# Running prompt rows and sample rows half a layer out of step in a four-layer diffusion trunk

## The chip, the cores and the metric

The program runs on all 8 cores of one Trainium2 chip (two dies of four cores). Each core does the same work on its own rows with its own copy of the program. The time is that of the slowest core, in device microseconds (us), from its first to its last instruction.

An eight-core program has a second, slower state in some executions: the cores of one die, sometimes of both, show a lower granted TensorE clock and the time grows (here by 3 to 16%). Such runs are named slow below and are left out of every comparison.

## The reference, cut to what matters

Four layers act on two groups of rows that share all weights. Prompt rows attend only to prompt rows. Sample rows use their own rows and cached context tensors. Even layers mix with a short convolution beside a neighbourhood attention, odd layers with window pooling beside a latent attention. Every layer ends in an MLP with squared relu, and six modulation vectors per layer come from a matrix `ada_w`.

```python
def sq_relu_mlp(h, w1, w2):               # 1024 -> 4096 -> 1024
    a = jax.nn.relu(h @ w1)
    return (a * a) @ w2

for l in range(DEPTH):                    # DEPTH = 4
    sh1p, sc1p, g1p, sh2p, sc2p, g2p = ada_mod(s_ctx, ada_w[l], ada_b[l])
    sh1s, sc1s, g1s, sh2s, sc2s, g2s = ada_mod(s_lat, ada_w[l], ada_b[l])
    hp = modulate(yp, norm1_g[l], sh1p, sc1p)
    hs = modulate(ys, norm1_g[l], sh1s, sc1s)
    # ... mix_p from hp alone, mix_s from hs and the caches (cut) ...
    yp = yp + g1p * mix_p
    ys = ys + g1s * mix_s
    yp = yp + g2p * sq_relu_mlp(modulate(yp, norm2_g[l], sh2p, sc2p), mlp_w1[l], mlp_w2[l])
    ys = ys + g2s * sq_relu_mlp(modulate(ys, norm2_g[l], sh2s, sc2s), mlp_w1[l], mlp_w2[l])
```

The two groups never read one another. That is what lets one run ahead of the other. Per core there are 512 prompt rows and 1024 sample rows, held as three blocks of 512 tokens: block 0 is prompt, blocks 1 and 2 are sample.

## The kernel before: the parts that matter

The kernel lists all operations with what they read and write. A scheduler in Python then plays the program through with a modelled duration for each operation, and so fixes, when the program is built, the order of the instructions on every engine. The program gives each engine its list in that order, with waits on semaphores; nothing in it picks another order at run time. The modelled duration of a weight load is this:

```python
DMA_LAT = 1.9
...
            if nd.kind == "dma":
                dma_free = max(dma_free, st + 1.0) + nd.nbytes      # one queue; nbytes holds us
                fin = dma_free + self.DMA_LAT - 1.0
...
        def DMA(q, pairs, reads, writes, sem, out=False, key=None):
            fns = [lambda h, o=o, i_=i_: h.dma_start(out=o, in_=i_) for (o, i_) in pairs]
            t = sum(R(o).nbytes() / (0.17e6 if R(o).dtype != R(i_).dtype else 0.25e6) for (o, i_) in pairs)
```

Weights lie in HBM as float32 and are cast to bfloat16 by the DMA. A tile of 1 MB (as it lands) thus costs 6.2 us of modelled queue time plus 1.9 us of latency. A tile goes to a slot; a slot is filled again only when all readers of its last contents are done:

```python
            def fill(self, srcs, after=(), key=None):
                self.b = P.renew(self.b)
                s = "ws%d" % (nsl[0] % 24)
                nsl[0] += 1
                DMA("pool", [(self.w[:, 0:src.shape[1], c0:c0 + nc_], src) for (c0, nc_, src) in srcs], list(after), [self.b], s, key=key)
                return self.w, self.b

        WT = [Slot(w=sb("WT%d" % s, (128, 8, 512), BF16)) for s in range(2)]
```

Where the plan leaves TensorE idle for more than 0.9 us, the scheduler puts in matmuls on a tile of ones, called fillers here, which are meant to keep its clock up:

```python
            if e == "pe" and self.warm is not None and st - free[e] > self.WARM_MIN:      # 0.9 us
                self.fill_gap(nodes, free[e], st, bank_free, bank_users)
```

All three blocks go through each layer together. In the MLP one fetched tile serves all three, and hidden values are squared on ScalarE (ACT) and masked on VectorE (DVE):

```python
            order = [M[0], M[1], WT[0], WT[1]] * 3 + [WT[0], WT[1], M[0], M[1]]
            ...
                    for tb in range(3):
                        for j in range(4):
                            ...
                            MMK(pt[:], [(w[:, kc, j * 128:(j + 1) * 128], hT[:, kc, blk(tb)]) for kc in range(8)],
                                [bw] + bh[tb], [pt.b])
                            mk, bm = msk.next()
                            ACT(mk[:], pt[:], AF.Square, [pt.b], [bm])
                            STT(hq[:, jj, blk(tb)], pt[:], 0.0, mk[:], ALU.is_gt, ALU.mult, [pt.b, bm], [bhq[jj][tb]])
...
        for l in range(depth):
            if l % 2:
                odd_layer(l, ada[l][1])
            elif l > 0:
                even_layer(l)
            mlp(l, l + 1 == depth, ada[l + 1][0] + (ada[l + 1][1] if l % 2 else []))
```

`MMK` is a group of eight accumulating matmuls, `STT` a DVE operation with a scalar and two tensors, `TT` and `TS` DVE operations with two tensors and with scalars.

## Time and profile before

| | before |
|---|---|
| fast runs (us) | 2498.53, 2502.76 (and 2496.78 beside the changed kernel) |
| slow run (us) | 2726.35 |
| spans of the cores in the profiled run | 2478.9 to 2500.3 |
| mean granted TensorE clock of the cores | 0.983 to 0.990 |
| weight tiles of the MLP, 1 MB each | 64 |
| fillers | 1095 |
| bytes moved by DMA | 212.01 MB |

These lines are from the page of the slowest core: busy time of TensorE, its busy share and that of ACT and of the DMA engines in 40 slices (9 means 90% or more), the DMA total, and the chain of work that ended last, as shares of the span.

```profile
PE 2345.9 (94%) x14913; PEld 1166.4 (47%) x14913; DVE 1183.4 (47%) x1748; ACT 1070.9 (43%) x1607; POOL 256.6 (10%) x344
...
PE   4999899999998899999999988999998879999999
...
ACT  2666741121567764111256774121136777412210
...
DMA  9969673333217758667534549343322391433322
...
DMA packets 204842, 212.01 MB, mean 85 GB/s; under 512 B 46320, under 2 KB 191472, under 8 KB 202736
...
PE 79%; DMA 9%; ACT 5%; issue 3%; DVE 2%; POOL 1%; ACTq 0%; POOLq 0%; DVEq 0%; SPq 0%
```

TensorE (PE) looks full. The rows below tell more: where ACT shows 5 to 7 (the attention of each layer) PE drops to 8 or 7 and the DMA row swings between 1 and 9; where ACT shows 1 to 2 (the MLPs) PE is at 9, and in the MLPs of layers 0, 2 and 3 the DMA is down to 2 to 4.

Three stretches of core 1 show the contrast. The columns are the stretch, its length, busy time and instruction count of each engine, the granted clock, the DMA share and GB/s.

```profile
core 1: us, PE busy (x) PEld busy (x) DVE busy (x) ACT busy (x) POOL busy (x), PEclk, DMA share, GB/s
400.00:425.00 25.00, 25.00 (x146) 11.78 (x145) 10.32 (x17) 2.98 (x5) 1.62 (x2) 1.00 0.47 75
800.00:825.00 25.00, 21.99 (x378) 14.97 (x375) 8.54 (x16) 22.38 (x26) 2.63 (x3) 1.00 0.82 164
875.00:900.00 25.00, 21.77 (x268) 13.06 (x266) 5.60 (x8) 23.77 (x25) 0.00 (x0) 1.00 0.01 1
```

The first is MLP: PE is full and nothing else is. The third is attention in layer 1: ACT is busy 23.77 of 25 us, PE waits for it, and the DMA is idle. The change wants to fill the third kind with work of the first.

### The profile page before, as it was taken

How to read it: one execution, taken by the hardware profiler on the slowest of the kernel's cores; microseconds unless marked ns; L12 is line 12 of the kernel's file. 1: busy time of each engine (PE TensorE's matmuls, PEld its weight loads, DVE VectorE, ACT ScalarE, POOL GpSimd, SP SyncE). 2: the span in 40 equal slices, each digit the busy share in tenths (PEclk: the TensorE clock that was granted, in tenths of full speed). 3: DMA queues.
4: the chain of work that ended last, by engine and by line, in shares of the span. 5: the costliest groups of instructions: out<-in, count | busy, mean ns of one | idle time of the engine just before them, and what ended most of it. 6: DMA issues, size and time to landing. Idle time of an engine off the chain costs nothing.

```text
span 2500.3 us, 39661 instructions; the slowest of 8 cores (2478.9 to 2500.3 us)
## 1 busy us (share of the span) xinstructions
PE 2345.9 (94%) x14913; PEld 1166.4 (47%) x14913; DVE 1183.4 (47%) x1748; ACT 1070.9 (43%) x1607; POOL 256.6 (10%) x344
## 2 busy tenths in 40 slices
PE   4999899999998899999999988999998879999999
PEld 3454444444445544444444544444444455444444
DVE  2556554444656245444465655444455533544443
ACT  2666741121567764111256774121136777412210
POOL 3200100000014000000031001000001310000000
PEclk9999999999999999999999999999999999999999
DMA  9969673333217758667534549343322391433322
GB/s 172 166 92 195 108 113 61 51 51 51 74 36 125 130 78 109 85 84 97 63 76 54 122 87 136 57 61 51 51 57 70 62 158 40 67 52 52 52 45 101
DMA packets 204842, 212.01 MB, mean 85 GB/s; under 512 B 46320, under 2 KB 191472, under 8 KB 202736
## 3 DMA queue, kind: packets, MB, share of 16 engines
q0 software_dynamic: 176992, 148.39, 43.6%
q1 hardware_dynamic: 27664, 61.09, 7.6%
q8 instruction: 123, 2.02, 0.3%
q14 instruction: 63, 0.52, 0.1%
HBM read 334.07 MB, written 22.15 MB: 142 GB/s over the span
## 4 chain that ended last, share of the span: by engine, by line
PE 79%; DMA 9%; ACT 5%; issue 3%; DVE 2%; POOL 1%; ACTq 0%; POOLq 0%; DVEq 0%; SPq 0%
PE psall L638 79%; ACT arena L662 3%; DMA yT<-ada_w 3%; DMA WT<-even_w_out 1%; DMA WT<-even_w_in 1%; DMA WT<-ada_w 1%; DMA yT<-odd_w_in 1%; DMA arena<-ada_w 1%; DVE ntmp L684 1%; POOL rtmp L673 1%; DVE arena L673 1%; DMA yT<-xT 1%; ACT rstd L662 1%; ACT hT L662 1%; PE psall L646 0%
## 5 line engine op out<-in xcount | busy, mean ns | idle before, releaser
L662 ACT ACTIVATE arena<-psall 128x512 f32<-128x512 f32 (+6 forms) x675 | 434.7, 651 | 1043.4 <-PE psall L638 1033.5
L638 PE MATMUL psall<-arena,WT 128*128 128x512 bf16 x2688 | 587.5, 380 | 10.4 <-DMA WT<-even_w_out 6.7
L638 PE MATMUL psall<-hT,arena 128*128 128x512 bf16 x2520 | 559.3, 382 | 7.2 <-ACT hT L662 7.2
L684 DVE SCALAR_TENSOR_TENSOR yT<-psall,mod,yT 128x512 f32<-128x512 f32 x480 | 359.3, 750 | 428.0 <-PE psall L638 427.8
L638 PE MATMUL psall<-arena 128*128 128x65 bf16 (+7 forms) x3272 | 470.2, 293 | 44.0 <-ACT arena L662 24.2
L684 DVE SCALAR_TENSOR_TENSOR arena<-psall,arena 128x512 bf16<-128x512 f32 x384 | 265.3, 691 | 400.1 <-ACT arena L662 399.7
L638 PE MATMUL psall<-hT,WT 128*128 128x512 bf16 x1872 | 424.9, 382 | 5.8 <-ACT hT L662 4.3
L638 PEld LDWEIGHTS psall<-arena,WT 128*128 128x128 bf16 x2688 | 262.7, 98 | 326.3 <-issue 12.8
L638 PEld LDWEIGHTS psall<-hT,arena 128*128 128x128 bf16 x2520 | 246.9, 98 | 306.2 <-issue 17.0
L638 PEld LDWEIGHTS psall<-arena 128*128 128x128 bf16 (+1 forms) x3272 | 237.5, 99 | 249.9 <-issue 77.9
L638 PEld LDWEIGHTS psall<-hT,WT 128*128 128x128 bf16 x1872 | 181.8, 98 | 218.4 <-issue 12.4
L662 ACT ACTIVATE arena<-psall,rk 128x1024 bf16<-128x1024 f32 x160 | 166.7, 1118 | 34.9 <-PE psall L638 34.4
L684 DVE SCALAR_TENSOR_TENSOR ntmp<-yT,A,nrstd 128x512 f32<-128x512 f32 x192 | 135.9, 746 | 20.6 <-ACT nrstd L662 14.0
L662 ACT ACTIVATE hT<-ntmp,mod 128x512 bf16<-128x512 f32 x176 | 121.4, 718 | 40.9 <-DVE ntmp L684 40.1
L662 ACT ACTIVATE nsq<-yT 128x1024 bf16<-128x1024 f32 x55 | 58.0, 1055 | 165.7 <-PE psall L638 113.0
L684 DVE SCALAR_TENSOR_TENSOR arena<-psall,cst_sb,rstd 64x512 bf16<-64x512 f32 (+1 forms) x90 | 67.3, 748 | 64.7 <-ACT rstd L662 62.6
L726 POOL DMA_DIRECT2D WT<-mlp_w x32 | 28.2, 881 | 541.8 <-PE psall L638 541.5
L726 POOL DMA_DIRECT2D arena<-mlp_w x32 | 28.2, 880 | 539.1 <-PE psall L638 532.6
L1535 PE MATMUL psall<-ones 128*128 128x128 bf16 x1095 | 71.1, 222 | 0.0
L662 ACT ACTIVATE rstd<-rstd 128x512 f32<-128x512 f32 (+2 forms) x92 | 64.7, 703 | 8.5 <-ACT rstd L662 0.4
L638 PE MATMUL psall<-hT,yT 128*128 128x512 bf16 x288 | 68.0, 379 | 0.0
L1535 PEld LDWEIGHTS psall<-ones 128*128 128x128 bf16 x1095 | 65.4, 99 | 4.7
(111 smaller groups left out, 1285.9 us busy)
## 6 DMA issues: line engine op xcount, KB each, us to landing
arena<-mlp_w POOLq DMA_DIRECT2D x32, 1024.0 KB, 10.5
WT<-mlp_w POOLq DMA_DIRECT2D x32, 1024.0 KB, 9.9
yT<-ada_w POOLq DMA_DIRECT2D x24, 1024.0 KB, 11.7
arena<-ada_w POOLq DMA_DIRECT2D x22, 1024.0 KB, 16.7
arena<-rpbx SPq DMA_DIRECT2D x64, 240.0 KB, 2.8
ysc<-yT SPq DMA_DIRECT2D x5, 2048.0 KB, 6.8
yT<-ysc SPq DMA_DIRECT2D x10, 1024.0 KB, 7.6
yT<-xT SPq DMA_DIRECT2D x3, 2048.0 KB, 14.7
```

What stands on the lines that cost most here:

```text
L638: h.matmul(R(out), lhsT=lhsT, rhs=rhs, start=start, stop=stop, skip_group_check=skip))
L662: return lambda h: h.activation(out=R(out), in_=R(in_), func=func, **kw)
L673: P.add(eng, [lambda h: h.tensor_tensor(out=R(out), in0=R(in0), in1=R(in1), op=op)], reads, writes, vdur(fsize(out), eng, isb(out, in0, in ...
L684: P.add("dve", [lambda h: h.scalar_tensor_tensor(out=R(out), in0=R(in0), scalar=scalar, in1=R(in1), op0=op0, op1=op1)], reads, writes, vdu ...
L726: fns = [lambda h, o=o, i_=i_: h.dma_start(out=o, in_=i_) for (o, i_) in pairs]
L1535: P.warm = lambda h, o: h.matmul(o, lhsT=ones[:, :], rhs=ones[:, :], start=True, stop=True)
```

## The change

Its intent: the prompt runs half a layer ahead. In phase A of a layer the sample's attention runs beside the prompt's output projection and half of the prompt's MLP (320 matmuls of 512 columns, 68 us at the 212 ns of the trace, PE work that needs little of ACT). In phase B the sample catches up with its projection and its MLP, and the next layer's prompt projections and attention run beside the second half of that. One fetched MLP tile can no longer serve all three blocks in the first two quarters, so those are fetched twice.

The core of the diff, with cuts marked by dots:

```diff
-        for l in range(depth):
-            if l % 2:
-                odd_layer(l, ada[l][1])
-            elif l > 0:
-                even_layer(l)
-            mlp(l, l + 1 == depth, ada[l + 1][0] + (ada[l + 1][1] if l % 2 else []))
+        for l in range(depth):
+            if l == 0:
+                e, Hp = even_first()
+            else:
+                e, Hp = (odd_sample if l % 2 else even_sample)(l, p)     # these call phase_a
+            p = phase_b(l, odd_src if l % 2 else even_src(e), Hp)
 ...
+        def phase_a(l, src_p):
+            T = l * 200
+            out_proj(l, [0], src_p, T - 0.5 if l else 20, zone=[6, 7])
+            Hp = hidden(Arena(0), [0])
+            slots = [WT[0], WT[1]] * 4
+            eA, eB = [], []
+            if l % 2 and l + 1 < depth:
+                X = Slot(Arena(4096))
+                ADA["slot"] = lambda nt: X
+                eA, eB = ada[l + 1]
+            for qd in range(2):
+                mlp_q(l, qd, [0], Hp, slots, T + 30 + qd, zone=[6, 7], tmr=ntr, extra=eB if qd else eA)
+            return Hp
 ...
+        def phase_b(l, src_s, Hp):
+            T = l * 200 + 100
+            out_proj(l, [1, 2], src_s, T)
 ...
+                if nxt_odd:
+                    par = Arena(8848)
+                    PW, PB = Slot(par), Slot(par, n=160)
+                    ADA["slot"] = lambda nt: PW
+                    eA, eB = ada[l + 1]
+            mlp_q(l, 2, [0, 1, 2], H, slots, T + 10, extra=eA + eB[:1],
+                  tmr=None)
 ...
+            mlp_q(l, 3, [0, 1, 2], H, slots, T + 20, extra=eB[1:], tail=tail_p)
 ...             (the next layer's prompt projections and attention, keys T + 21 to T + 28)
+            mlp_q(l, 0, [1, 2], H, slots, T + 30)
+            mlp_q(l, 1, [1, 2], H, slots, T + 40, tail=tail_s)
```

Two smaller parts travel with it. The squared relu is computed in another way, and the scheduler may not let the backlog of weight loads grow beyond 10 modelled us:

```diff
-                            mk, bm = msk.next()
-                            ACT(mk[:], pt[:], AF.Square, [pt.b], [bm])
-                            STT(hq[:, jj, blk(tb)], pt[:], 0.0, mk[:], ALU.is_gt, ALU.mult, [pt.b, bm], [bhq[jj][tb]])
+                            RELU(pt)          # in place in PSUM, on ACT or DVE, whichever the plan has free
+                            ACT(hq[:, half * 4 + j, :], pt[:], AF.Square, [pt.b], [bhq[half * 4 + j]])
 ...
+    DMA_AHEAD = 10.0
 ...
+                    if nd.kind == "dma" and nd.nbytes > 1.0 and dma_free - self.DMA_AHEAD > st:
+                        st = dma_free - self.DMA_AHEAD
```

The prompt's own half MLP uses a third form, a `max` on DVE and a product on DVE or POOL. Small rotary products may go to either of DVE and POOL, and more token blocks are spilled to HBM and reloaded.

## The prediction

> **What bounds the kernel now.** TensorE, but less tightly than its 94% busy share says. In the MLP stretches (365-668, 985-1275, 1580-1870, 2210-2480 us of the windows view) 117-118 matmuls of 512 columns start in 25 us: one per 212 ns, granted clock 1.00. Nothing can be gained there. The Trainium skill ("TensorE: Matmul & The Clock Gate", Back-to-back issue gap) gives N/2.4 + 2.5 ns for an isolated gap; the trace agrees within 2%. "Trainium Kernel Development and Optimization" (Performance Expectations) warns that matmul busy time is a bad metric; here too: at 825-850 us PE is 22.3 us busy, yet streams only 16.3 us of columns.
>
> Pricing every matmul of the trace at columns/2.4 GHz (27 ns at least), the program streams 2206 us; fillers (the 1095 matmuls on a tile of ones) cost another 59 us of otherwise idle PE. So 294 of 2500 us are not useful streaming. About 70 lie before 90 us (first weights) and 6 at the end. The other ~218 us lie in the mixers: ~41 us in layer 0 (175-375), ~63 in layer 1 (668-985), ~36 in layer 2 (1400-1580), ~75 in layer 3 (1870-2210). There ACT paces (87.7 of 105 us at 800-905; 1.118 us per exp of 128x1024 against ~0.67 us of matmuls), norm chains leave gaps, and the chain of waits shows DMA stalls of 9-20 us on ada_w, even_w_out and odd_w_in.
>
> **What the change does.**
> - Matmul work is unchanged: 2206 us.
> - Each sample attention gets the prompt's out-projection (64 matmuls, 14 us) and half its MLP (256 matmuls, 55 us) as filler: ~69 us of independent PE work per layer, against 36-75 us lost there. The next layer's prompt projections and attention go beside the sample's MLP.
> - Squared relu becomes relu in PSUM, then square: two passes as before, ~0.6-0.7 us each against 1.7 us of matmuls; free.
> - Weights are fetched again: 32 MLP tiles, 8 out-projection tiles, and layers 1-3's mixer weights for two groups: ~54 MB more, plus ~16 MB of spill and reload. Moved bytes 212 -> ~280 MB, DMA share 51% -> ~66%. A 1 MB tile costs ~7 us when the DMA is saturated (~150 GB/s, 825-850 us).
> - Worst stage: layer 1's mixer, with 8 MLP, 2 out, 12 ada tiles and the mixer's own: I estimate ~215 us of DMA against ~225 us of PE. Late tiles stall the fixed order of PE there.
>
> **On the critical path.** Of the ~218 us I expect ~125 recovered: filler covers attention and norm gaps, but DMA lateness and transitions leave ~90 us (25 per mixer in layers 0, 1 and 3, 15 in layer 2). Start and end stay ~75 us. 2206 + 75 + 92 = 2373 us, 5% faster. Range 2310 to 2445. Faster by over 2%: 0.89; within 2%: 0.08; slower: 0.03.
>
> **What would show it.** Useful streaming unchanged at ~2206 us; fillers fall from 1095 to under 600; no stretch where ACT is nearly full while PE streams under 70%; 512-column matmuls still every 212 ns in the MLP; mlp_w issues 64 -> 96; DMA share near 66%. In the chain of waits, ACT's 5% falls below 3%; DMA keeps at least its 9%, which now makes most of the loss. PE in the chain: 79% -> over 84%.
>
> **What would make it wrong.** (a) DMA late under 30% more bytes: the PE order is fixed, so the filler itself stalls attention; then 2430 or more. (b) A two-bank PSUM zone and two weight slots for the prompt's MLP throttle the filler. (c) The denser PE is granted a lower clock. (d) Better: gaps really vanish and residual falls to 40 us: 2320.

## More of the kernel before

What PE waited for on core 1 (us in total, number of waits, the longest):

```profile
PE psall L638 <- ACT arena L662: 25.7, 85, 1.8
PE psall L638 <- DMA WT<-ada_w: 24.5, 2, 17.9
...
PE psall L638 <- DMA arena<-ada_w: 8.3, 4, 3.9
PE psall L638 <- DMA yT<-ada_w: 6.5, 6, 1.9
```

The 24.5 us on `WT<-ada_w` are the first weights of the program; every kernel below has them. Added up over the whole list, PE waited 42.1 us for ACT, 50.3 us for DMA, 23.0 us for DVE and 14.5 us for GpSimd (POOL). Last, how long a weight tile took from its issue to its landing on the slowest core (count, size, median us):

```profile
arena<-mlp_w POOLq DMA_DIRECT2D x32, 1024.0 KB, 10.5
WT<-mlp_w POOLq DMA_DIRECT2D x32, 1024.0 KB, 9.9
yT<-ada_w POOLq DMA_DIRECT2D x24, 1024.0 KB, 11.7
```

The order of the instructions was planned for 8.1 us of an unloaded queue; this becomes the main point later. For an unloaded queue that is not far off: of the 106 tiles of `mlp_w` and `ada_w` that core 1 issued after 100 us, 40 had no other transfer in flight and landed in 8.7 us (median). The other 66 took 12.1 us, and one in ten of those 19 us or more.

## The result, and the profile after

| | before | after |
|---|---|---|
| fast runs (us) | 2496.78, 2498.53, 2502.76 | 2540.97, 2542.30 |
| slow runs (us) | 2726.35 | 2785.65, 2880.91 |
| spans of the cores in the profiled run | 2478.9 to 2500.3 | 2469.3 to 2539.4 |
| granted clock of the cores | 0.983 to 0.990 | 0.971 to 0.983 |
| MLP weight tiles, 1 MB each | 64 | 96 |
| fillers | 1095 | 716 |
| bytes moved by DMA (MB) | 212.01 | 285.63 |

The changed kernel is right, and slower: the ratio is 1.0169, with a 95% interval of 1.0139 to 1.0199. A ratio here is the mean time of one kernel's fast runs over that of the other's fast runs of the same rounds, so it is not quite the ratio of the medians that are quoted. That is within 2%, but the interval excludes any gain, and the prediction was 2373 us.

The same lines of the page, slowest core again:

```profile
PE 2326.9 (92%) x14291; PEld 1151.0 (45%) x14534; DVE 1020.7 (40%) x1550; ACT 1219.2 (48%) x1848; POOL 322.5 (13%) x412
...
PE   5879889989899988999999998999999999899998
...
ACT  2536744243555667424443775153156376852322
...
DMA  9975896669566688734696966965976636353352
...
DMA packets 279703, 285.63 MB, mean 112 GB/s; under 512 B 70240, under 2 KB 264544, under 8 KB 276064
...
PE 70%; DMA 20%; issue 3%; ACT 3%; DVE 2%; POOL 1%; another core or an unknown queue 0%; DVEq 0%; ACTq 0%; POOLq 0%; SPq 0%
```

ACT's work is spread more evenly, as intended: its row seldom falls to 1 now. The DMA row has lost its long stretches of 3. In the chain, DMA went from 9% to 20%, and PE from 79% down to 70%. (This core's trace lacks 243 matmul records, 14291 against 14534 weight loads; sums are therefore taken from core 1.)

Core 1, four stretches, columns as before:

```profile
core 1: us, PE busy (x) PEld busy (x) DVE busy (x) ACT busy (x) POOL busy (x), PEclk, DMA share, GB/s
850.00:875.00 25.00, 17.76 (x124) 8.48 (x122) 11.34 (x21) 5.17 (x9) 4.85 (x7) 0.86 1.12 224
950.00:975.00 25.00, 18.40 (x246) 11.41 (x247) 2.66 (x6) 20.66 (x21) 0.87 (x1) 0.91 0.84 121
1050.00:1075.00 25.00, 25.00 (x118) 11.29 (x117) 0.00 (x0) 17.09 (x29) 0.87 (x1) 1.00 0.31 43
1400.00:1425.00 25.00, 25.00 (x117) 11.33 (x116) 20.74 (x30) 22.40 (x37) 5.26 (x6) 1.00 1.44 175
```

The last line is the change as it was meant: ACT busy 22.4 of 25 us and PE full, with 117 matmuls of 512 columns. The first is what came with it: PE, ACT, DVE and POOL all far from full, the clock down to 0.86, and the DMA saturated (I read shares above 1 as saturated). Of the 94 stretches of 25 us between 100 and 2450 us of core 1, 15 had a DMA share of 0.85 or more before; after, 31 of 95 have.

What PE waited for on core 1, and how long tiles took to land on the slowest core:

```profile
PE psall L641 <- DMA WT<-ada_w: 25.4, 2, 18.3
PE psall L641 <- DMA WT<-mlp_w: 24.7, 6, 7.4
PE psall L641 <- DMA arena<-ada_w: 23.9, 17, 4.2
PE psall L641 <- ACT arena L665: 19.9, 53, 3.4
PE psall L641 <- DMA arena<-odd_w_in: 10.9, 4, 3.1
```

```profile
WT<-mlp_w POOLq DMA_DIRECT2D x64, 1024.0 KB, 10.8
arena<-ada_w POOLq DMA_DIRECT2D x38, 1024.0 KB, 13.4
arena<-mlp_w POOLq DMA_DIRECT2D x32, 1024.0 KB, 10.6
```

The medians to landing are little above those of before. What grew is the number of tiles that share the queue: on core 1, counted as before, 115 of 138 in place of 66 of 106. They took 11.7 us in the median (one in ten 19 us or more), the 23 others 8.6 us.

Over the whole list the waits for DMA grew from 50.3 to 103.8 us, while those for ACT fell from 42.1 to 29.5 us. The eight cores agree: this sum is 73.1 us on core 5, which has the shortest span (2469.3 us), and 129.6 us on core 0, which has the longest (2539.4 us). One such wait in full, from the timeline of core 1 (start, duration, engine, instruction; in brackets the idle time before it and what ended it):

```profile
850.47 0.94 POOL L739 DMA_DIRECT2D WT<-mlp_w  x1 [2.68 <-PE psall L649]
...
860.14 0.61 PE L649 MATMUL psall<-ident,arena 128*128 128x128 bf16 x8
...
860.96 0.87 POOL L739 DMA_DIRECT2D WT<-mlp_w  x1 [2.20 <-PE psall L649]
...
867.51 1.86 PE L641 MATMUL psall<-hT,WT 128*128 128x512 bf16 x4 [6.76 <-DMA WT<-mlp_w]
```

A tile of the prompt's MLP, the filler of the plan, is issued at 850.47. PE runs out of other work at 860.75 and reads the tile at 867.51, 17 us after the issue. The plan counts 8.1 us for a tile that need not queue. PE's list is fixed, so the attention work behind those matmuls waits too: the filler has become the stall.

To see all of the loss I paired the starts of successive matmuls on core 1, took columns/2.4 GHz + 2 ns as the useful part of each interval (27 ns at least), and put the rest down to the clock or to what ended the wait. The time of fillers is the whole time until the next useful matmul starts. (The two kernels with thin tiles and with the slower plan are experiments, below; the rest, some 35 us of each, is start, end and gaps too small to assign.)

| us on core 1 | before | after | after, thin tiles | after, slower plan |
|---|---|---|---|---|
| useful streaming | 2214 | 2214 | 2214 | 2214 |
| fillers | 121 | 79 | 73 | 122 |
| slow clock | 32 | 45 | 10 | 20 |
| waits for ACT | 36 | 27 | 27 | 32 |
| waits for DVE and POOL | 30 | 24 | 21 | 25 |
| waits for DMA | 24 | 87 | 10 | 25 |

The change as a whole, the new relu included, did give back time: fillers −42 us, ACT −9 us, POOL and DVE −6 us. Waits for DMA took 63 us of it and the slower clock 13 us. Core 1 is 15 us longer as a result; the slowest core (core 0) 39 us longer.

### The profile page after: what moved, and what is told of

Read it like the earlier page. It is cut to its first block, busy times and chain, and to the rows that moved or that the text cites. A ratio compares the mean times of both kernels' runs of the same rounds, so it can differ in the third digit from the quotient of the medians.

```text
span 2539.4 us, 38663 instructions; the slowest of 8 cores (2469.3 to 2539.4 us)
## 1 busy us (share of the span) xinstructions
PE 2326.9 (92%) x14291; PEld 1151.0 (45%) x14534; DVE 1020.7 (40%) x1550; ACT 1219.2 (48%) x1848; POOL 322.5 (13%) x412
## 2 busy tenths in 40 slices
DMA packets 279703, 285.63 MB, mean 112 GB/s; under 512 B 70240, under 2 KB 264544, under 8 KB 276064
## 4 chain that ended last, share of the span: by engine, by line
PE 70%; DMA 20%; issue 3%; ACT 3%; DVE 2%; POOL 1%; another core or an unknown queue 0%; DVEq 0%; ACTq 0%; POOLq 0%; SPq 0%
PE psall L641 70%; DMA arena<-ada_w 8%; DMA WT<-mlp_w 3%; DMA yT<-even_w_in 2%; ACT arena L665 2%; DMA arena<-rpbx 2%; DMA arena<-odd_w_in 1%; DMA WT<-ada_w 1%; DMA yT<-ada_w 1%; DMA arena<-PA 1%; DVE arena L676 1%; DMA WT<-even_w_out 1%; ACT rstd L665 1%; DMA nak_out<-arena 0%; POOL rtmp L676 0%
## 5 line engine op out<-in xcount | busy, mean ns | idle before, releaser
L641 PE MATMUL psall<-arena,WT 128*128 128x512 bf16 x2866 | 657.2, 383 | 19.8 <-DMA WT<-mlp_w 12.8
L665 ACT ACTIVATE arena<-psall 128x512 bf16<-128x512 f32 (+7 forms) x631 | 411.3, 659 | 230.3 <-PE psall L641 181.5
L665 ACT ACTIVATE psall<-psall 128x512 f32<-128x512 f32 x320 | 186.4, 582 | 483.4 <-PE psall L641 482.8
L641 PE MATMUL psall<-arena 128*128 128x65 bf16 (+8 forms) x2940 | 368.6, 275 | 27.8 <-ACT arena L665 17.3
L641 PE MATMUL psall<-hT,WT 128*128 128x512 bf16 x1462 | 344.3, 387 | 27.4 <-DMA WT<-mlp_w 15.0
L641 PEld LDWEIGHTS psall<-arena 128*128 128x128 bf16 (+1 forms) x2960 | 200.8, 98 | 189.3 <-issue 45.3
L641 PEld LDWEIGHTS psall<-hT,WT 128*128 128x128 bf16 x1504 | 146.8, 99 | 202.7 <-issue 42.1
L665 ACT ACTIVATE arena<-psall,rk 128x1024 bf16<-128x1024 f32 (+1 forms) x224 | 196.9, 934 | 74.2 <-PE psall L641 68.8
L641 PE MATMUL psall<-hT,yT 128*128 128x512 bf16 x697 | 167.5, 385 | 17.8 <-DMA yT<-even_w_in 14.7
L641 PEld LDWEIGHTS psall<-hT,yT 128*128 128x128 bf16 x704 | 68.7, 99 | 99.2 <-issue 24.1
L691 DVE SCALAR_TENSOR_TENSOR arena<-psall,cst_sb,rstd 64x512 bf16<-64x512 f32 (+2 forms) x102 | 76.3, 749 | 82.2 <-ACT rstd L665 70.9
## 6 DMA issues: line engine op xcount, KB each, us to landing
WT<-mlp_w POOLq DMA_DIRECT2D x64, 1024.0 KB, 10.8
arena<-ada_w POOLq DMA_DIRECT2D x38, 1024.0 KB, 13.4
```

Of the source, the lines that this page charges most:

```text
L641: h.matmul(R(out), lhsT=lhsT, rhs=rhs, start=start, stop=stop, skip_group_check=skip))
L665: return lambda h: h.activation(out=R(out), in_=R(in_), func=func, **kw)
L691: P.add("dve", [lambda h: h.scalar_tensor_tensor(out=R(out), in0=R(in0), scalar=scalar, in1=R(in1), op0=op0, op1=op1)], reads, writes, vdu ...
```

## The experiments

My theory after the comparison: the order of work is good, but weights come late under the added bytes, and a fixed order turns each late tile into a stall of PE. Rivals: (1) one slot for all `ada_w` tiles, which has each load wait for the last reader, is the cause (B in the texts); (2) the structure itself is slow, with two PSUM banks and two slots for the prompt's MLP, whatever the DMA does; (3) the new bound on the backlog of loads delays them; (4) the refetched tiles cost more than the filler they feed brings (the contrary, that the filler is worth more, is F in the texts). Times are medians of the fast runs; times of different chips differ by some 0.3%, so ratios to the kernel before decide.

### Take the bytes away: e1_thin_refetch, e2_thin_ada, e3_thin_all

In these a chosen tile's load moves only the first of its eight row groups (128 KB), and the matmuls read that group eight times. The modelled cost, and so the order of every instruction, stays the same. The results are wrong.

```diff
+        # e1: n is ignored, thin marks the prompt's own out-projection and MLP tiles
+        # e2: thin marks ada_w tiles; e3: every tile; both leave the first seven as they are
+        THINNED = lambda thin, n: n > 7                           # e3
             def fill(self, srcs, after=(), key=None, thin=False):
 ...
+                if THINNED(thin, nsl[0]):
+                    P.nodes[-1].fns = [lambda h, o=self.w[:, 0:1, c0:c0 + nc_], i_=src[:, 0:1]: h.dma_start(out=o, in_=i_) for (c0, nc_, src) in srcs]
+                    return self.w[:, 0:1].broadcast_to(list(self.w.shape)), self.b
```

> Wrong result on purpose: the changed kernel, same instruction order, but the ten weight tiles per layer that are fetched a second time for the prompt alone (its out-projection and half its MLP) move one eighth of their bytes. Theory A (TensorE stalls because the extra traffic makes weight tiles late): about 35 MB less is moved, the time falls from 2541 to 2450-2480 us, and waits on ada_w shrink too. Theory B (what is late is the modulation weights, because they now go through one slot, whatever the traffic): no more than 25 us are gained, the mlp_w waits alone. Theory C (the new order is paced by ACT, DVE and PSUM, not by DMA): within 10 us of the changed kernel.

> Wrong result on purpose: the changed kernel, same order, but all modulation tiles (ada_w) after the first four move one eighth of their bytes. Theory A: about 38 MB less, so much the same gain as for the thin refetch, 2450-2480 us. Theory B: the ada_w waits vanish, 40-70 us gained, clearly more than by the thin refetch. Theory C: within 10 us of the changed kernel.

> Wrong result on purpose: the changed kernel, same order, but every weight tile after the first seven moves one eighth of its bytes, so hardly any is late. Theories A and B: all DMA waits and the slow clock after them go, 90-130 us gained, 2410-2450 us, and the slowest core comes within 1% of the fastest. Theory C: at most 40 us gained.

| | median us | ratio to before | 95% interval | MB moved |
|---|---|---|---|---|
| after | 2541 | 1.0169 | 1.0139 to 1.0199 | 285.63 |
| e1, prompt's own tiles thin | 2486.70 (one slow run of four) | 0.9919 | 0.9887 to 0.9951 | 248.93 |
| e2, ada tiles thin | 2454.45 | 0.9782 | 0.9758 to 0.9806 | 245.26 |
| e3, all tiles thin | 2398.14 | 0.9556 | 0.9531 to 0.9582 | 120.25 |

With late weights taken away the same order of instructions takes 143 us less by the fast runs and 145 between the two profiled runs (2540.97 and 2396.14); I use 145 below (by the ratios, which allow for the chips, it is 153). The chain and the landing of a tile in e3:

```profile
PE 86%; DMA 5%; ACT 4%; DVE 2%; issue 2%; POOL 1%; DVEq 0%; ACTq 0%; SPq 0%; POOLq 0%
...
WT<-mlp_w POOLq DMA_DIRECT2D x64, 128.0 KB, 3.0
```

DMA falls from 20% of the chain to 5% (of which 1.7% is the attention bias tables, which are not thinned, and 2% the first weights), and PE rises to 86%. The cores end within 12 us of each other (2382.7 to 2394.5) where they spread over 70 us, and every core has a clock of 0.992 or more. On core 1 the span falls by 120 us, and the table above says where: 77 us of waits for DMA and 35 us of slow clock.

Also, e1 and e2 take away 37 and 40 MB and bring 54 and 87 us (63 and 97 by the ratios), together about as much as e3. If their gains add, which no run here tests, the other 88 MB that e3 takes away bring next to nothing: the bytes of these tiles count, and not the total. Of the forecasts, A's ranges were nearest: e1 fell just short of its range, e2 fell in it, and e3 gained more than any theory said; but e2 gained clearly more than e1, as B has it. C falls. Rival 2 falls as it is put, whatever the DMA does: two slots and two banks do not hold the prompt's MLP back once tiles land in 3.0 us; no wait for `WT<-mlp_w` is among the larger waits of e3. With full tiles the two slots may still share in the lateness, for a load waits for its slot; no run gives the prompt's MLP more of them. A caveat: thin tiles also mean repeated weight values, and the data may bear on the clock. Dense MLP stretches run at 1.00 with full tiles too, so I put little on it. And the chip of e1 to e4 adds a little: the clock records of these profiles have, besides 1 and 0.5, the value 0.8125, mostly on cores 4 to 7, for at most 115, 76, 29 and 137 us in e1 to e4 (so 5 us of lost clock in e3 and 26 in e4), where the profiles of before and after have 1 and 0.5 alone. In us these four gains are thus too small rather than too large.

### One slot for ada tiles: e4_ada_two_slots

The modulation tiles of every next layer go through two slots, all in phase B. The results are right.

```diff
-            if l % 2 and l + 1 < depth:            # phase A
-                X = Slot(Arena(4096))
-                ADA["slot"] = lambda nt: X
-                eA, eB = ada[l + 1]
 ...
-                    ADA["slot"] = lambda nt: PW     # phase B, even l
-                    eA, eB = ada[l + 1]
+                x = Arena(4096)
+                XS = [Slot(x), Slot(x)]
+                ADA["slot"] = lambda nt: XS[nt % 2]
+                eA, eB = ada[l + 1]
```

> Right result: the modulation weights of the next layer go through two slots instead of one, and always beside the half of the MLP that all rows share (also after layer 1, where they lay in the attention stage before). Theory B: the ada_w waits (27-44 us by core) fall by more than half, 30-60 us gained, about 2490 us, faster than the kernel before. Theory A: 0-25 us gained, from moving traffic out of layer 1's attention. Theory C: no change within 10 us.

Measured: fast runs of 2517.81, 2520.56 and 2529.18 us, ratio 1.0051 (1.0017 to 1.0085). It gains 20 to 30 us, a part of the 87 that thin ada tiles bring. The run changes two things at once, the number of slots and the stage in which the loads of layer 2's tiles run, and it lies between what A and B said. So the single slot is at most a part of the loss; rival 1 falls as the main cause.

### Tell the scheduler the truth: e5_slow_model, g1_lat_only, f5_slower_model

If late weights are the cause, a plan that knows they are late should put other work first. These change only the modelled cost of a load; the program's work is the same and the results are right.

```diff
-    DMA_LAT = 1.9
+    DMA_LAT = 3.4                                  # e5;  g1: 5.0;  f5: 4.5
-            t = sum(R(o).nbytes() / (0.17e6 if ...
+            t = sum(R(o).nbytes() / (0.14e6 if ...  # e5;  g1: left at 0.17e6;  f5: 0.12e6
```

> Right result, same work: only the numbers by which the program's list scheduler plans DMA are changed (a cast tile takes 7.5 instead of 6.2 us, and lands 1.5 us later), nearer to the 10-13 us from issue to landing of the traces. Theory P (planning: TensorE's fixed order puts weight uses earlier than the weights can land): at least half of the 145 us that the thin tiles gained comes back, 2440-2480 us. Theory Q (physical: the tiles cannot come sooner, through few slots and a DMA near saturation): at most 25 us gained, the stalls turn into planned fillers, 2515-2545 us.

> Right result: the changed kernel, the scheduler's tile still takes 6.2 us but lands 3.1 us later. If what was too hopeful is the latency: 2475-2500 us, as much as the rate and latency together (2483 us). If it is the rate under load, since a backlog of tiles adds up: 2510-2535 us.

> Right result: the changed kernel, the scheduler's DMA slower again: 8.7 us for a cast tile and 2.6 us more to land than in the changed kernel. If planning still gains: 2450-2475 us. If the rest is physical, waits only turn into fillers: 2475-2500 us.

| | planned us for an unqueued 1 MB tile | median us | ratio | 95% interval | fillers |
|---|---|---|---|---|---|
| after | 8.1 | 2541 | 1.0169 | 1.0139 to 1.0199 | 716 |
| g1 | 11.2 | 2492.23 | 0.9967 | 0.9946 to 0.9988 | 1042 |
| e5 | 10.9 | 2482.75 | 0.9932 | 0.9912 to 0.9952 | 1121 |
| f5 | 13.2 | 2521.80 (one slow run of four) | 1.0125 | 1.0059 to 1.0191 | 2010 |

The planned time is 1 MB over the modelled rate plus the latency. With a plan near the measured 10 to 13 us the changed kernel gains 58 us, 40% of the 145, with the same bytes. That is short of the half that theory P asked for, and more than twice what Q allowed. The chain of e5:

```profile
PE 83%; DMA 7%; ACT 4%; issue 2%; DVE 2%; POOL 1%; ACTq 0%; DVEq 0%; POOLq 0%
```

g1 shows that the latency alone brings most of it. f5, slower than both its forecasts, shows the limit: with a plan slower than the chip, PE hardly waits for DMA any more (29.4 us in all on core 1, most of that the start), but 2010 fillers stand where the waits were. A cautious plan does not make bandwidth; it turns an unplanned stall into a planned gap, and gains only where other work can be moved into it. The table of losses shows the same trade for e5: waits for DMA go from 87 to 25 us, and fillers take 43 us more.

### Both together: e8_two_slots_slow

This is e4 and e5 in one kernel.

> Right result: two slots for the modulation weights beside the shared half of the MLP, and the slower DMA in the scheduler. Theory P: the two add, 2430-2465 us, faster than the kernel before by over 1%. Theory Q: near the two slots alone, 2505-2530 us.

Measured: 2510.51 us, ratio 1.0041 (1.0017 to 1.0066), worse than e5 alone by 28 us. The two gains don't add. The plan has 1527 fillers, where e5 has 1121 and e4 727. That all ada tiles in phase B crowd that phase, and that the plan, now knowing it, answered with fillers, is my reading and not shown.

### The same two measures on the kernel before: e6_slow_model_before, e7_before_thin

These are the controls: the slower plan of e5, and the thin tiles of e3, in the kernel before.

> Right result: the kernel before, with the same slower DMA in its scheduler. Control for the run above. Theory P: gains too, but less, for its DMA waits on TensorE are about 25-35 us: 2475-2495 us. Theory Q: no change, 2495-2510 us.

> Wrong result on purpose: the kernel before, same order, every weight tile after the first seven moves one eighth of its bytes. What the interleaving is worth when DMA is free is the difference to the changed kernel treated so (2396 us). If the idea works as meant and only DMA ate the gain: 2440-2475 us here, so 45-80 us of gain. Rival (the changed order is no better at filling TensorE, whatever the DMA does): 2390-2410 us here.

Measured: e6 2486.36 us (two slow runs of six), ratio 0.9946 (0.9928 to 0.9963); e7 2464.26 us, ratio 0.9856 (0.9834 to 0.9877). The kernel before loses about 36 us to late weights where the changed one loses 145, and a truer plan brings it some 14 us where it brings the changed one 58. So lateness is not a constant of the program: the change made it about four times as dear with 1.35 times the bytes (285.63 over 212.01 MB).

### Is the refetch worth it: e9_one_quarter_l0, e10_one_quarter

On top of e5, only one quarter of the prompt's MLP runs beside the sample's attention, in layer 0 only (e9) or in all layers (e10). Each such layer fetches four tiles fewer.

```diff
+        NQ = lambda l: 1 if l == 0 else 2          # e9;  e10: lambda l: 1
-            for qd in range(2):
+            for qd in range(NQ(l)):
 ...
+            if NQ(l) == 1:
+                mlp_q(l, 1, [0, 1, 2], H, slots, T + 5, extra=eA)
 ...
```

> Right result: the slower DMA in the scheduler, and in layer 0 the prompt takes only one quarter of its MLP beside the sample's attention (four weight tiles less are fetched twice). Layer 0's mixer has most of the planned fillers that are left (about 36 of 88 us after the start). Theory T (the second fetch itself is what layer 0 cannot afford, physically): 10-25 us under the slower scheduler's 2483 us. Theory F (the filler work is worth more than the four tiles cost): 0-15 us above it.

> Right result: as the run before, one quarter in all four layers: 16 MB less fetched twice, and half the filler in each attention stage. Theory T: 25-45 us under 2483 us. Theory F: 5-30 us above it, with the ACT gaps on TensorE growing from about 32 to over 45 us.

Measured: e9 2492.22 us, ratio 0.9948 (0.9896 to 1.0000), by the interval not to be told apart from e5 (0.9932); by the times, on the same chip, it is 9 us above e5, as theory F said. e10 has two fast runs, 2526.78 and 2527.51 us, and four slow ones; ratio 1.0087 (1.0006 to 1.0168), about 40 us over e5. Its one profile is of a slow run and is not used. Giving filler away in all layers to save bytes loses, by more than F said: rival 4 falls, at least for this amount.

### The bound on the backlog: e11_no_ahead

```diff
-    DMA_AHEAD = 10.0
+    DMA_AHEAD = 1e9
```

> Right result: the changed kernel without the new bound on how far DMA issues run ahead (a part of the change). If that bound makes tiles late: 15 us or more faster than 2541 us. If it is what keeps urgent tiles in front: 15 us or more slower. I expect within 15 us.

Measured: fast runs from 2543.62 to 2550.2 us, ratio 1.0161 (1.0079 to 1.0243). No difference from 1.0169 shows, within some 20 us either way, and no run is faster than the changed kernel's. Rival 3 falls as the main cause.

### The relu alone: e12_before_relu, f3_after_old_relu

The new squared relu is put into the kernel before (e12), and taken out of the changed one (f3, where the MLP quarters with sample rows get the old form; the prompt's own quarters keep theirs). Both are right.

```diff
-                            mk, bm = msk.next()                                  # e12, in the kernel before
-                            ACT(mk[:], pt[:], AF.Square, [pt.b], [bm])
-                            STT(hq[:, jj, blk(tb)], pt[:], 0.0, mk[:], ALU.is_gt, ALU.mult, [pt.b, bm], [bhq[jj][tb]])
+                            RELU(pt)
+                            ACT(hq[:, jj, blk(tb)], pt[:], AF.Square, [pt.b], [bhq[jj][tb]])
```

> Right result: the kernel before with only the new squared relu (relu in PSUM on ACT or DVE, then square on ACT). My prediction called it free: within 5 us of the kernel before. Rival: the added ACT work delays hidden tiles, over 15 us slower.

> Right result: the changed kernel with the old squared relu (square on ACT, then a masked multiply on DVE) for all tiles but the prompt's early ones. If the relu works here as in the kernel before: 20-45 us slower than 2541 us, so the rest of the change costs about 76 us. If the interleaving had already filled the gaps that the relu fills: within 12 us of 2541 us, so the rest of the change costs about 40 us.

Measured: e12 2465.76 us (2461.68 to 2470.74), ratio 0.9843 (0.9789 to 0.9896); no right version has a lower median, and it beats both kernels. (The interval is wide because the kernel before had one odd run of 2527.23 us, still counted as fast.) f3 has fast runs of 2581.14 and 2589.13 us and two slow ones, ratio 1.0321 (1.0298 to 1.0344). So the small part of the change is worth about 38 us in the kernel before (37 by the medians, 39 by the ratio) and about as much (1.0321 − 1.0169, or 38 us of 2503) in the changed one. The changed kernel, slower as a whole, contains a gain of 1.5%, hidden under a larger loss. My forecast for e12, within 5 us, was a miss; f3 came out as its first branch said.

Why it gains can be read where a mixer ends and the MLP begins. From the timeline of the kernel before, core 1:

```profile
955.27 2.56 PE L1535 MATMUL psall<-ones 128*128 128x128 bf16 x43
956.04 0.75 DVE L684 SCALAR_TENSOR_TENSOR ntmp<-yT,A,nrstd 128x512 f32<-128x512 f32 x1 [0.37 <-ACT hT L662]
...
956.71 0.68 DVE L684 SCALAR_TENSOR_TENSOR arena<-psall,arena 128x512 bf16<-128x512 f32 x1
...
957.31 1.40 DVE L684 SCALAR_TENSOR_TENSOR ntmp<-yT,A,nrstd 128x512 f32<-128x512 f32 x2
...
959.67 4.69 PE L638 MATMUL psall<-hT,arena 128*128 128x512 bf16 x21 [1.84 <-ACT hT L662]
```

DVE alternates between the norm of the next block (`ntmp`, 0.75 us) and the masked product of the last block's hidden tiles (`arena<-psall,arena`, 0.68 us). PE runs 43 fillers and waits, 4.4 us in all, for the norm to give it `hT`. With the new form the relu can go to ACT, and DVE is left with the norm. The same transition in windows of 20 us, first in the kernel before and then in e12 (columns as above):

```profile
950.00:970.00 20.00, 18.16 (x145) 9.92 (x144) 10.87 (x18) 10.97 (x18) 3.50 (x4) 1.00 1.03 143
```

```profile
940.00:960.00 20.00, 20.00 (x95) 9.08 (x93) 7.52 (x12) 16.38 (x29) 1.75 (x2) 1.00 0.73 106
```

DVE falls from 10.87 to 7.52 us, ACT rises from 10.97 to 16.38, and PE is full with 95 real instructions where it had 145 that include the 43 fillers. The trace before has such runs of fillers at the start of the MLP in all four layers (at about 339, 955, 1549 and 2163 us). DVE alternates in the same way in each, but the wait does not end with the norm in each: in layers 0 and 2 it ends with a tile of `ada_w`. The first real matmuls after the fillers, in layers 0, 2 and 3:

```profile
342.58 0.99 PE L638 MATMUL psall<-sTb,arena 128*128 128x2 bf16 x32 [2.21 <-DMA arena<-ada_w]
...
1554.61 0.99 PE L638 MATMUL psall<-sTb,arena 128*128 128x2 bf16 x32 [3.87 <-DMA arena<-ada_w]
...
2168.65 1.78 PE L638 MATMUL psall<-hT,arena 128*128 128x512 bf16 x4 [2.25 <-ACT hT L662]
```

In e12 none of the four is left, and the fillers fall from 1095 to 891. The accounting of the table above, done for e12 on core 1, gives 95 us for fillers in place of 121 and 17 us of slow clock in place of 33; the waits move by some 3 us each. The four transitions held about 21 us of the filler time, and 7 us of slow clock in or just after them. So they are some 27 of the 37 us by which core 1 is shorter. That DVE alone is the reason, with `ada_w` late in two of the four, is argued and not shown.

### Can more be had: f1_before_relu_thin, f2_before_relu_slow, f6_before_best

These build on e12: with thin tiles (f1, wrong), with the slower plan of e5 (f2), and with that and the rotary products free to go to DVE or POOL (f6).

> Wrong result on purpose: the kernel before with the new squared relu, all weight tiles after the first seven at one eighth of their bytes. The changed kernel so treated takes 2396 us, the kernel before 2464 us. If the interleaving is what gained with free DMA: 2445-2464 us here. If most of the 68 us was the relu: 2415-2435 us here, so that the interleaving itself is worth only 20-40 us.

> Right result: the kernel before with the new squared relu and the slower DMA in its scheduler. If the two gains (38 and 14-17 us) add: 2440-2455 us, over 2% faster than the kernel before. If the relu's gain was luck of one schedule: 2470-2490 us.

> Right result: as f2, and the small rope multiplications may run on DVE or GpSimd, as in the changed kernel. TensorE's gaps behind GpSimd were 10-15 us in the kernel before and 2 us in the changed one: 5-12 us faster than f2, 2430-2448 us. Rival: no difference, they only move to DVE.

Measured: f1 2442.19 us, ratio 0.9751 (0.9736 to 0.9765). f2 2469.95 us (one slow run of four), ratio 0.9859 (0.9839 to 0.9879). f6 2468.79 us (two slow runs of five), ratio 0.9859 (0.9842 to 0.9875). The slower plan adds nothing to e12, though it brought some 14 us without the new relu; I had expected the two gains to add, and that was a miss. Put the other way round, the relu brings only 16 us (22 by the ratios) where the slower plan is already in (e6 to f2), and 22 us (26 by the ratios) where weights are in time (e7 to f1). So its 38 us belong to this plan; a part of them is time that punctual weights or another plan win as well. Freeing the rotary products does nothing either.

f1 completes the account. It puts the worth of the interleaving, with weights always in time, at 2442 − 2396 = 46 us:

| step | us | from |
|---|---|---|
| before | 2502 | |
| new relu | −37 | before to e12 (2465) |
| interleaving, weights in time | −46 | f1 (2442) to e3's profiled run (2396) |
| late weights, beyond what e12 loses to them | +122 | (2541 − 2396) − (2465 − 2442) |
| after | 2541 | |

The sum closes by construction; what it tells is the sizes, of which the first two rest on two measured kernels each and the third on four. They depend on the order of the steps: with weights in time the relu is worth 22 us, not 37.

## Why the prediction was wrong, point by point

- **Useful streaming unchanged, 212 ns for a 512-column matmul: right.** It is 2214 us on core 1 in both kernels by the same count (the prediction has 2206; pricing the trace again at its own price, columns/2.4 GHz and 27 ns at least, gives 2195, which is 0.5% less and changes little below), and dense stretches show 117 to 118 matmuls in 25 us, 212 to 214 ns each. The Trainium skill ("TensorE: Matmul & The Clock Gate", Back-to-back issue gap) gives 216 ns for the isolated gap, which the trace meets within 2%.
- **Tiles, bytes and DMA share: right.** `mlp_w` loads went from 64 to 96, bytes to 285.63 MB (predicted about 280), the share of the DMA engines from 51% to 67% (predicted 66%).
- **ACT no longer paces: right for the most part.** The fullest stretch of ACT was 23.77 of 25 us with PE at 21.77; after, it is 22.40 with PE at 25.00. ACT's share of the chain fell from 5% to 3%. But two stretches are left with ACT busy over 20 of 25 us and PE streaming less than 70% of the time: 250 to 275 us (14.9 us of columns) and 950 to 975 us (14.0 us).
- **Fillers under 600: wrong, 716.** **PE over 84% of the chain: wrong, 70%.** "DMA keeps at least its 9%" was true and far too mild: it is 20%.
- **"Squared relu becomes relu in PSUM, then square … free": wrong, in the other direction.** It gains 38 us in either kernel. I counted passes per hidden tile and found them equal; I did not look at which engine the pass leaves, and what that engine does at the start of each MLP.
- **The step that failed: "DMA lateness and transitions leave ~90 us (25 per mixer in layers 0, 1 and 3, 15 in layer 2)".** With start and end at 75 us as predicted, the loss beside useful streaming is 2541 − 2206 − 75 = 260 us in place of the 92 of the sum. Late weights are 145 of it (after against e3), and 115 remain with weights in time (2396 − 2206 − 75). Each of the two alone is larger than the one term that was to hold both. So even a perfect supply of weights would have given 2396 us, above the predicted 2373 though inside the range, and that already contains the gain from relu.
- **Why I mis-sized it.** I had the fact in hand: "~215 us of DMA against ~225 us of PE" in layer 1's mixer. I read it as "fits". From 850 to 1000 us of core 1, in layer 1's attention stage, the DMA share is 0.88 in the mean; the two `mlp_w` tiles issued between 848 and 870 us took 16.9 and 21.8 us to land, and the `ada_w` tile 18.3 us. A slot is refilled only after its last reader, so I take it that they could hardly be issued earlier; no run tests that. The Trainium skill ("DMA: Bandwidth & Descriptors", Measured) has 6.15 us and 341 GB/s for one 1 MB load with the pair's other core idle, and I priced a tile at 7 us. Both say how long the DMA engines are occupied. What stalls PE is issue to landing: 8.6 us with nothing else in flight, 10.8 and 13.4 us in the median over all tiles, and 17 us in the stall shown.
- **Of the four warnings, (a) came true as written, and the number with it:** "the PE order is fixed, so the filler itself stalls attention; then 2430 or more". I gave it too small a chance. (b) is not the cause (e3). (c) has it backwards: the clock fell to 0.971 to 0.983 where PE stalled more, and the denser e3 has 0.992 to 0.995. The Trainium skill ("TensorE: Matmul & The Clock Gate", Part 1: The HAM clock gate) has the clock gate lower the clock after idle time, and this agrees with it: the 25 us that hold the 6.76 us stall have a granted clock of 0.86, and slow clock on core 1 costs 32, 45, 10 us in before, after and e3, in the same order as the waits for DMA (24, 87, 10 us). In the clock records of core 1 these are pieces of 3.41 or 6.83 us at half speed, 85, 121 and 27 us in all.

What stays open: e5 recovers 58 of the 145 us by planning. Whether the other 87 can be had by a better order, with more slots, or only with fewer bytes in the mixers, no run here tells. Nor is it settled what the 115 us are that remain in e3; on core 1 the largest part is 73 us around fillers, gaps that the plan itself has, where the plan still counts on 8 us for a tile that then takes 3.

## What to carry to other kernels

When an order of instructions is fixed at build time, work moved in as filler brings its own loads, and each one that lands late stalls the very work it was to hide; so price a load by issue to landing in the busiest stage, not by occupied DMA time, and count a stage whose DMA and compute times are nearly equal as one that may run late. Give the planner the measured landing time before judging a new order by its result. And test each small rider of a large change alone: here a two-line change of the relu was worth 38 us in either kernel as planned, and alone it beat both.

## What the Trainium skill lacked or had wrong

- "DMA: Bandwidth & Descriptors", Measured: it gives the occupied span of one 1 MB load on one core (6.15 us), and the page has a fit for one DMA alone and the bandwidth left when both cores of a pair load, but no time from issue to landing with all eight cores loading and casting. Here that is 8.6 us in the median for a 1 MB bfloat16 tile cast from float32 with nothing else of its core in flight, 10 to 13 us over all such tiles, 17 us in the stall shown, and 3.0 us for a 128 KB tile when the rest of the traffic is thin.
- "TensorE: Matmul & The Clock Gate", Back-to-back issue gap: the page calls about 131 ns for each 512-column matmul the sustained figure and 216 ns only the isolated one. In the traces of before and after the sustained pace of dense 512-column matmuls is 212 to 214 ns.
- The same page, Part 1: it says that a die goes to 13/16 (0.8125) of the clock once three of its cores run dense matmuls, and stays there while the load lasts. Here all eight cores run dense matmuls, and in the fast profiles of before and after the means are 0.971 to 0.990 and the clock records have the values 1 and 0.5 alone. The value 0.8125 shows only in some executions, and there for part of the time or nearly all of it: for 636 to 782 us on cores 4 to 7 in the slow profile of e10, for up to 137 us in the fast profiles of e1 to e4, and, by the means (0.807 to 0.813 on cores 0 to 3, 0.971 to 0.979 on the other die), nearly throughout the 2880.91 us run of the changed kernel.
